# Letting three kinds of small products in a mixing phase wait for company on TensorE

## The chip, the cores and the metric

The kernel runs on one core of one Trainium2 chip, in one launch. The metric is device time in microseconds (us), as the median of several executions. The engines are named as in the profile: PE is TensorE, DVE is VectorE, ACT is ScalarE, POOL is GpSimd, SP is SyncE, which issues most DMAs. PEld is the load of a matrix product's stationary operand, which runs beside PE.

## The reference

Two layers of a diffusion backbone over 256 context and 512 latent tokens (768 columns together), with a model width of 1024, in float32. Each layer has a mixing sub-layer and a squared-ReLU MLP. Cut to what matters:

```
h = modulate(rmsnorm(x))
conv, q, k, v, rw, gate = split(h @ w_in)          # 7552 output channels
y_att  = differential attention(q, k, v)           # 4 heads
y_conv = silu(layernorm(depthwise_conv31(glu(conv))))
y_rw   = rwkv7(rw)                                 # 8 heads of 64, two directions
m = g1*(y_conv@p_conv) + g2*(y_att@p_att) + g3*(y_rw@p_rwkv);  x += gl1 * (m @ w_out)
x += gl2 * (square(relu(modulate(rmsnorm(x)) @ mlp_w1)) @ mlp_w2)
```

The RWKV-7 branch is a recurrence over tokens with a 64x64 state for each head and direction:

```
sa = s @ (-kk_t);  s = s * w_t + sa (kk_t * a_t)^T + v_t k_t^T;  y_t = s @ r_t
```

Its per-token decay w and rate a come from two low-rank products (64 rows in, 128 channels out).

## The kernel before, in words

**Wide products.** Every dense matrix is cut into units of 128 output channels. A float32 product is made of three products of rounded parts (weights `wh`, `wl`; activations `hh`, `hl`), all 128x128 stationary with 512 columns (latent) or 256 columns (context), into tiles called `mmps`. ACT makes `wh` from the loaded `wr`, DVE makes `wl`. Where this text counts wide products, one of 256 columns counts half.

**The recurrence, in chunks of 64 tokens.** For each of four head pairs and two halves of the tokens, `half_prep` makes decays and rates from the low-rank products (tiles `lps` and `aps`, two products each, of 64 rows). `half_t` makes the products that are masked into triangles (`tps`, three groups of eight per half, 64 rows). `inverse` takes the triangles through DRAM and inverts 16x16 blocks on DVE; `half_solve` joins the blocks to inverses of 64x64 (`wps`, `jps`, products of 32x32). `half_tok` transposes operands (`trps`, `vps`) and makes the value products (`tvps`, three groups of eight per half, 64x64). `chain_piece` then walks the chunks in order: `ca`, `cb` and `psy` are its small products (128x64 and 64x64), and each step waits for ACT and DVE between its products. All of these stand in PE's one queue, between wide products.

**What sets the order.** The program is written out engine by engine by a planner at build time. Each piece of work is a Python generator that yields the time at which its next instruction could start, its engine, and sometimes a lock on PSUM slots (`"bb"` wants both) and a time bonus. `weave` asks all open generators, takes the one with the earliest possible start, and adds the instruction's estimated cost to that engine's clock (`spend`). Ties go to the generator named first in an order string; in a mixing phase the wide products (`G`) stand behind the chain, preparation and token work. So a group of small products that was ready went in at the next boundary between two wide products.

**Stages of a layer.** The mixing phase (`phase_a`) runs until chain, inverse, preparation and token work have ended; wide products of the input projection fill PE meanwhile. Then attention (`attend`) follows: scores `sps`, softmax on DVE and ACT, transposes `atps`, values `mmps<-aat`, a norm over `ash`/`asl`, the result split in `yah`/`yal`. What is left of the input projection (the gates last) fills PE there. In layer 0 the convolution's 124 taps (`cacc`, on DVE) run in and behind attention, in layer 1 in the mixing phase. Then come the merges (`ya`, `y`, `yc` times the p matrices), `w_out` and the MLP. In layer 0 much of the gates is left for the time behind attention; in layer 1 the last of the input projection ends with attention.

Of the kernel before, what the change touches and what calls it, by code (L numbers as in the profile page):

```python
# [19 lines left out]
P = 128  # L20
# [31 lines left out]
SPARE = 1.5  # L52
EPS = 0.02
STICK = 0.2
BLK = 1040
CTX = (0, NCTX)
LAT = (NCTX, NLAT)
# [63 lines left out]
class Trunk:  # L121
# [105 lines left out]
    def product(self, out, lhsT, rhs, at=None, beside=0, **kw):  # L227
        self.nc.tensor.matmul(out, lhsT, rhs, **kw)  # L228
        m, n = lhsT.free_size(), rhs.free_size()
        c = n if rhs.dtype == F32R else 4 * n * max(m, 32) / P  # L230
        cost = (max(0.027, c / 2400) + 0.003) if not beside else 0.004
        if rhs.dtype != F32R:
            cost = max(cost, 0.1 if m == P else 0.0) + (0.012 if 32 < n <= P else 0.04 if n > P else 0.0)
        if self.short and m == P:
            cost += 0.06
        self.short = cost < 0.1
        return self.spend("PE", cost, at)

    def turn(self, out, src):
        self.nc.tensor.transpose(out, src, self.ident)  # L240
        return self.spend("PE", 0.119)

    def load(self, out, in_, q=None, rate=360e3):
# [39 lines left out]
    def weave(self, order, streams, until=None):  # L283

        todo = self.todo
        todo += [[g, 0.0, "PE", None, None, 0.0, k] for k, g in streams.items()]
        todo.sort(key=lambda s: order.find(s[6]) % 99)  # L290
        while todo and not (until and until()):
            best, at = None, 0.0
            for s in todo:
                held, names = self.held(s[4])
                if held is None or s[3] and not s[3]():
                    continue
                t = max(s[1], self.clock[s[2]] + s[5], held) - s[5]
                if best is None or t < at - EPS:
                    best, at, got, since = s, t, names, held
            assert best, "no stream can go on"  # L300
            self.t0 = max(best[1], since)
            self.now = max(self.now, at)
            self.got = got[0] if got else None
            for k in got:
                self.locks[k] = None
            try:
                y = next(best[0])
            except StopIteration:
                todo.remove(best)
                continue  # L310
            best[1:6] = y + (None, None, 0.0)[len(y) - 2:]
# [100 lines left out]
    def start(self):  # L412
        self.queues, self.closing, self.n_queued = [], False, 0
        self.plan, self.after, self.after_over, self.n_after = [], deque(), False, 0
        self.n_load = self.n_conv = self.n_used = 0
        self.banks = dict(lat=deque([0.0, 0.0]), ctx=deque([0.0]))
        self.ring = dict(lat=deque([self.mm, self.mm]), ctx=deque([self.mm]))
        self.gone = dict(lat=deque(), ctx=deque())
        self.raws, self.parts = deque([self.wp] * WR), deque([self.wp] * WC)
        self.locks, self.t0, self.now, self.todo, self.short = {}, 0.0, 0.0, [], False  # L420
        self.shared, self.shared_t = 0, 0.0

    def enqueue(self, i, q):
# [550 lines left out]
    def half_prep(self, l, p, hh):  # L974
# [8 lines left out]
        t3 = max(pp["kk_t"], pp["r_t"], pp["lw_t"], self.ready["lw"], self.ready["la"])  # L983
        late = bk[:, 1].rearrange("p c x t -> p (c x t)")
        low = []
        for i, (name, src) in enumerate((("e1", self.lw), ("a", self.la))):
            yield t3, "PE", None, "bb"
            pss = self.both_slots("lps" if i == 0 else "aps")
            for d in range(2):
                rows = slice(64 * d, 64 * d + 64)  # L990
                e = self.product(pss[d][:, 0:N], pp["lora_w"][rows, i, :], src[rows, u0:u0 + N], beside=d, start=True, stop=True)
            for d in range(2):
                yield e, "ACT"
                x = late[:, N * i:N * i + N] if d else pr.tile([P, N], F32, tag=name, name=name)
                o = 8 * i + 4 * d + p
                t = S.activation(out=x, in_=pss[d][:, 0:N], func=AF.Tanh, scale=0.5, bias=self.wa0[:, o:o + 1])
                self.free(f"b{d}", t)
                low.append((x, t))
        for d in range(2):
# [48 lines left out]
            t3 = V.tensor_tensor(out=bet, in0=q64(a), in1=q64(e3), op=ALU.mult)  # L1048
# [3 lines left out]
            for tok, n, more in add:  # L1052
# [7 lines left out]
                if more:  # L1060
                    t = V.tensor_tensor(out=dst, in0=dst, in1=src, op=ALU.add)
                else:
                    t = S.activation(out=dst, in_=src, func=AF.Copy)
# [3 lines left out]
    def half_t(self, n, pp, hh, prep, c0):  # L1067
        pr, V = self.pr, self.V
        ar, bk, pc, ready = prep
        ta = pr.tile([P, 6, 2, 2, 64], F32, tag="ta", name="ta", bufs=2)  # L1070
        trs = []

        def masked(b, ps, pi, h, e, tr):

            yield e, "DVE"
            t = V.tensor_tensor(out=ta[:, 2 * pi:2 * pi + 2, h, :, :], in0=ps[:, :, :, 0:64],
                                in1=self.mask[:, 0:1, :].unsqueeze(1).to_broadcast([P, 2, 2, 64]), op=ALU.mult)
            if tr is not None:
                yield e, "DVE"
                t = V.tensor_tensor(out=tr[:, :, :, h, :].rearrange("p c g t -> p (c g) t"),  # L1080
                                    in0=ps.rearrange("p c g t -> p (c g) t")[:, :, 64:128],
                                    in1=self.mask[:, 1, :].unsqueeze(1).to_broadcast([P, 4, 64]), op=ALU.mult)
            self.free(b, t)
            return t

        for pi in range(3):
            need_y = 128 * (3 * hh + pi) >= c0
            nx = 2 if need_y else 1
            tr = pr.tile([P, 2, 2, 2, 64], F32, tag="tr", name="tr", bufs=6 if c0 == 0 else 4) if need_y else None
            trs.append(tr)  # L1090
            yield ready, "PE", None, "bb"
            pss = [x.rearrange("p (c g t) -> p c g t", c=2, g=2) for x in self.both_slots("tps")]
            for cc in range(2):
                c = 2 * pi + cc
                for d in range(2):
                    g = 1 - (cc ^ d)
                    for h in range(2):
                        hs = slice(64 * h, 64 * h + 64)
                        e = self.product(pss[h][:, cc, g, 0:64 * nx], bk[hs, d, c].rearrange("p x t -> p (x t)"),
                                         ar[hs, d, c, 0:nx].rearrange("p x t -> p (x t)"), beside=h, start=True, stop=True)  # L1100
            for h in range(2):
                t = yield from masked(f"b{h}", pss[h], pi, h, e, tr)
        sc, sc2 = self.blk_in[self.blk % 2], self.blk_out[self.blk % 2]
        self.blk += 1

        def blocks(x):
            return x.rearrange("(p x) -> p x", x=BLK)[:, 0:1024].rearrange("p (i w) -> p i w", w=64)[:, :, 0:16]

        def rows(x, g):
            return x[g * 48 * BLK:(g + 1) * 48 * BLK].rearrange("(n y) -> n y", y=4 * BLK)[:, 0:4096].rearrange(  # L1110
                "n (s t) -> s n t", t=64)

        yield t, "SP"
        for g in range(2):
            td = self.load(rows(sc, g), ta[64 * g:64 * g + 64, :, :, g, :].rearrange("p c h t -> p (c h) t"), rate=180e3)
        for d in range(2):
            for x in range(2):
                tb = self.G.tensor_tensor(out=bk[:, d, :, x, :], in0=bk[:, d, :, x, :],
                                          in1=pc[:, d, :].unsqueeze(2).to_broadcast([P, 6, 64]), op=ALU.mult)
        j = pr.tile([P, 6, 2, 64], F32, tag="j", name="j", bufs=2)  # L1120
        st = dict(hh=hh, ta=ta, bk=bk, ar=ar, pc=pc, trs=trs, toks=[], tok_t=[], gvs=[], tvs=[], j=j, pp=pp, bk_t=tb, ta_t=t)
        self.inverses.append((st, td, lambda x=sc: blocks(x), lambda x=sc2: blocks(x), lambda g, x=sc2: rows(x, g)))
        return st
# [28 lines left out]
    def half_tok(self, st, pi):  # L1152
# [9 lines left out]
        t = S.activation(out=tok.rearrange("p d c t -> p (d c t)"), in_=ps, func=AF.Copy)  # L1162
# [12 lines left out]
        t = S.activation(out=gv[64:128, 1:3, :], in_=pv[64:128], func=AF.Copy)  # L1175
        st["gvs"].append(gv)
        self.free(b, t)
        yield t, "PE", None, "bb"
        pss = [self.rwe.tile([P, 512], F32, tag=f"b{g}", name="tvps", bufs=1) for g in range(2)]
        for cc in range(2):  # L1180
            for h in range(2):
# [9 lines left out]
        for g in range(2):  # L1191
            gr = slice(64 * g, 64 * g + 64)
            t = S.activation(out=tv[gr].rearrange("p c t -> p (c t)"), in_=pss[g][gr, 0:256], func=AF.Copy)
# [1050 lines left out]
```

## Time and profile before

| | |
|---|---|
| median of 3 runs | 2925.59 us (2921.22 to 2925.92) |
| the profiled execution's own time | 2913.63 us |
| its span, first to last instruction | 2911.8 us |
| PE busy | 2768.5 us, 95% of the span |
| DVE busy | 1961.5 us, 67% |
| ACT busy | 1299.9 us, 45% |
| mean granted TensorE clock | 0.986 |

The profiled execution took 12 us less than the median of the timed runs, so differences are worked out against 2913.63 us and then carried over to the median. A busy share is that of the whole span; the stages have different limits. PE's busy time counts a product from its start to the end of its pipeline, so what a product costs is read from the distance between the starts of two neighbours.

### The profile page before, as it was taken

What the parts mean: (1) busy time and instruction counts of PE and PEld (TensorE: products, weight loads), DVE (VectorE), ACT (ScalarE), POOL (GpSimd) and SP (SyncE); (2) the same over time, 40 slices, a digit from 0 to 9 for tenths busy, and PEclk for the clock granted to TensorE, in tenths of its full rate; (3) what the DMA queues carried; (4) which work ended last, traced back from release to release, by engine and by line L of the source; (5) the groups of instructions that cost most, each with busy time, mean ns of one, the idle gap of its engine ahead of it and who ended that gap; (6) DMA issues with size and microseconds to landing.
All of it is one profiled execution on the core that took longest, in us unless ns stands there. A gap on an engine that the chain in (4) does not pass through costs nothing.

```text
span 2911.8 us, 56372 instructions
## 1 busy us (share of the span) xinstructions
PE 2768.5 (95%) x22423; PEld 2229.7 (77%) x22423; DVE 1961.5 (67%) x4311; ACT 1299.9 (45%) x2522; POOL 104.9 (4%) x181
## 2 busy tenths in 40 slices
PE   8999999999999999999999999999999888899998
PEld 6777777777788887888888777777777656788887
DVE  6778787489995548764333569889985667644445
ACT  4556655455544224231313356556554653433333
POOL 0000000011000000000000000000000100000000
PEclk9999999999999999999999999999999999999999
DMA  5232223354237633553112223223245535322223
GB/s 210 65 77 70 74 79 90 115 151 127 72 124 271 242 119 120 183 186 101 63 62 69 96 70 86 66 83 83 73 120 155 146 119 160 130 97 96 95 95 104
DMA packets 247751, 330.96 MB, mean 114 GB/s; under 512 B 118256, under 2 KB 124032, under 8 KB 247360
## 3 DMA queue, kind: packets, MB, share of 16 engines
q1 hardware_dynamic: 242160, 311.63, 33.6%
q0 software_dynamic: 3712, 14.17, 2.0%
q8 instruction: 176, 2.88, 0.4%
q10 hardware_dynamic: 1616, 1.56, 0.2%
q14 instruction: 87, 0.71, 0.1%
HBM read 266.32 MB, written 47.60 MB: 108 GB/s over the span
## 4 chain that ended last, share of the span: by engine, by line
PE 73%; DVE 14%; ACT 4%; DMA 3%; issue 2%; SPq 0%; DVEq 0%; POOL 0%; ACTq 0%; POOLq 0%
PE mmps L228 60%; PE ca L228 3%; DVE cacc L92 2%; DVE wl L92 2%; DVE ast L92 2%; PE tps L228 1%; ACT wh L92 1%; PE psy L228 1%; PE jps L228 1%; PE wps L228 1%; PE tvps L228 1%; DVE ap L92 1%; DVE x L92 1%; PE atps L240 1%; PE sps L228 1%
## 5 line engine op out<-in xcount | busy, mean ns | idle before, releaser
L228 PE MATMUL mmps<-hh,wh 128*128 128x512 f32 (+1 forms) x2344 | 850.0, 363 | 22.1 <-DVE k L92 5.7
L228 PE MATMUL mmps<-hh,wl 128*128 128x512 f32 (+1 forms) x2344 | 843.3, 360 | 6.0 <-DVE wl L92 5.9
L228 PE MATMUL mmps<-hl,wh 128*128 128x512 f32 (+1 forms) x2344 | 843.6, 360 | 4.3 <-DVE hl L92 4.1
L92 DVE TENSOR_TENSOR wl<-wr,wh 128x512 fp32r<-128x512 f32 x596 | 412.2, 692 | 473.9 <-ACT wh L92 460.1
L92 ACT ACTIVATE wh<-wr 128x512 fp32r<-128x512 f32 x596 | 375.2, 630 | 707.6 <-PE mmps L228 656.9
L228 PEld LDWEIGHTS mmps<-hh,wh 128*128 128x128 f32 x2344 | 446.9, 191 | 93.4 <-issue 18.1
L228 PEld LDWEIGHTS mmps<-hh,wl 128*128 128x128 f32 x2344 | 446.1, 190 | 77.1 <-DVE wl L92 12.8
L228 PEld LDWEIGHTS mmps<-hl,wh 128*128 128x128 f32 x2344 | 447.3, 191 | 67.5 <-DVE hl L92 7.4
L228 PE MATMUL mmps<-ffl,wh 128*128 128x512 f32 (+1 forms) x792 | 279.3, 353 | 0.0
L228 PE MATMUL mmps<-ffh,wh 128*128 128x512 f32 (+1 forms) x792 | 278.1, 351 | 0.0
L228 PE MATMUL mmps<-ffh,wl 128*128 128x512 f32 (+1 forms) x792 | 277.1, 350 | 0.0
L92 DVE SCALAR_TENSOR_TENSOR cacc<-upad,dww,cacc 128x783 f32<-128x783 f32 (+1 forms) x240 | 215.1, 896 | 4.3
L228 PEld LDWEIGHTS mmps<-ffh,wh 128*128 128x128 f32 x792 | 149.1, 188 | 22.7
L228 PEld LDWEIGHTS mmps<-ffh,wl 128*128 128x128 f32 x792 | 148.9, 188 | 21.5
L228 PEld LDWEIGHTS mmps<-ffl,wh 128*128 128x128 f32 x792 | 149.4, 189 | 20.8
L92 DVE SCALAR_TENSOR_TENSOR x<-mmps,mod,x 128x512 f32<-128x512 f32 (+1 forms) x126 | 80.1, 636 | 46.2 <-PE mmps L228 44.8
L92 POOL TENSOR_TENSOR bk<-bk,pc 128x384 f32<-128x384 f32 x64 | 57.4, 927 | 1200.0 <-PE tps L228 1138.5
L92 DVE SCALAR_TENSOR_TENSOR sq<-mmps,rl 128x512 f32<-128x512 f32 x96 | 56.9, 596 | 40.0 <-ACT rl L92 39.9
L92 ACT ACTIVATE stage<-mmps 128x512 f32<-128x512 f32 (+1 forms) x116 | 59.1, 510 | 51.7 <-PE mmps L228 48.7
L92 ACT ACT_TABLE_LOAD x62 | 79.5, 1283 | 4.2 <-PE mmps L228 2.1
L92 ACT ACTIVATE rl<-mmps 128x512 f32<-128x512 f32 x96 | 49.3, 514 | 67.9 <-PE mmps L228 67.9
L92 DVE TENSOR_REDUCE ast<-sps 128x1 f32<-128x768 f32 (+1 forms) x80 | 67.5, 844 | 17.3 <-PE sps L228 17.3
(317 smaller groups left out, 4377.1 us busy)
## 6 DMA issues: line engine op xcount, KB each, us to landing
wr<-in_w_dram SPq DMA_DIRECT2D x268, 256.0 KB, 2.5
wr<-in_win_dram SPq DMA_DIRECT2D x236, 256.0 KB, 2.7
modw<-in_modw_dram SPq DMA_DIRECT2D x80, 512.0 KB, 4.6
wr<-in_pw_dram SPq DMA_DIRECT2D x48, 256.0 KB, 2.9
wr<-in_wo_dram SPq DMA_DIRECT2D x44, 256.0 KB, 2.6
g<-stage SPq DMA_DIRECT2D x24, 384.0 KB, 3.2
gate<-g SPq DMA_DIRECT2D x24, 384.0 KB, 3.8
scb<-in_modw_dram SPq DMA_DIRECT2D x16, 512.0 KB, 6.5
```

The lines of the kernel that those rows point to most:

```text
L92: f(**kw)
L228: self.nc.tensor.matmul(out, lhsT, rhs, **kw)
L240: self.nc.tensor.transpose(out, src, self.ident)
```

## The change

A new constant `DEFER = 1.5` (us). The three places that ask for both PSUM slots for low-rank (`lps`, `aps`), masked (`tps`) and value (`tvps`) products now yield `-DEFER` as their bonus. For a negative bonus `weave` takes the possible start as the ready time if PE's last planned product was a small one (`self.tiled`: fewer than 128 rows or columns of the stationary operand), and as the ready time plus 1.5 us otherwise. A wide product or a transpose clears `self.tiled`. A group that is late for any other reason by 1.5 us goes in as before. No instruction is added or removed by the diff itself; the planner writes another order.

```diff
+DEFER = 1.5
...
         self.short = cost < 0.1
+        self.tiled = m < P or lhsT.shape[0] < P
         return self.spend("PE", cost, at)
...
         self.nc.tensor.transpose(out, src, self.ident)
+        self.tiled = False
...
-                t = max(s[1], self.clock[s[2]] + s[5], held) - s[5]
+                if s[5] < 0:
+                    t = max(s[1] - (0.0 if self.tiled else s[5]), self.clock[s[2]], held)
+                else:
+                    t = max(s[1], self.clock[s[2]] + s[5], held) - s[5]
...
-            yield t3, "PE", None, "bb"
+            yield t3, "PE", None, "bb", -DEFER
...
-            yield ready, "PE", None, "bb"
+            yield ready, "PE", None, "bb", -DEFER
...
-        yield t, "PE", None, "bb"
+        yield t, "PE", None, "bb", -DEFER
```

**Place 1: PE, mixing phase of layer 0, the low-rank products of the fifth half (third head pair).** Before:

```order
L228 MATMUL tvps<-gv,ta 64x64 x8
L228 MATMUL mmps<-hh_177,wl 128x512
L228 MATMUL mmps<-hh_179,wh 128x512
L228 MATMUL mmps<-hl_180,wh 128x512
L228 MATMUL mmps<-hh_179,wl 128x512
L228 MATMUL lps<-lw,loraw 128x384 x2
L228 MATMUL mmps<-hh_181,wh 128x512
L228 MATMUL mmps<-hl_182,wh 128x512
```

With the change:

```order
L229 MATMUL mmps<-hh_177,wl 128x512
L229 MATMUL ca<-x_702,ar 64x128 x2
L229 MATMUL psy<-tr,gv 64x64
L229 MATMUL psy<-ar,x_701 64x64
...
L229 MATMUL lps<-lw,loraw 128x384 x2
L229 MATMUL ca<-rhs,j 64x64
L229 MATMUL cb<-rhs,j 64x64
...
L229 MATMUL mmps<-hh_179,wh 128x512
```

The low-rank pair stood alone between wide products and now stands inside a step of the chain.

**Place 2: PE, the end of attention in layer 1.** `aat` is the last value product, `ash`/`asl` the sum for the last head's norm, `yah` the first merge product. Before:

```order
L228 MATMUL mmps<-aat,avt 128x512 x6
L228 MATMUL mmps<-hl_17324,wh 128x512
L228 MATMUL mmps<-hh_17323,wl 128x512
L228 MATMUL mmps<-hh_17325,wh 128x512
L228 MATMUL mmps<-hl_17326,wh 128x512
L228 MATMUL mmps<-hh_17325,wl 128x512
L228 MATMUL mmps<-ash,onesr 128x512
L228 MATMUL mmps<-asl,onesr 128x512
L228 MATMUL mmps<-yah_25362,wh 128x512
```

With the change:

```order
L229 MATMUL mmps<-hh_17317,wh 128x512
L229 MATMUL mmps<-hl_17318,wh 128x512
L229 MATMUL mmps<-ash,onesr 128x512
L229 MATMUL mmps<-asl,onesr 128x512
L229 MATMUL mmps<-hh_17317,wl 128x512
L229 MATMUL mmps<-hh_17319,wh 128x512
...
L229 MATMUL mmps<-hl_17326,wh 128x512
L229 MATMUL mmps<-hh_17325,wl 128x512
L229 MATMUL mmps<-yah_25321,wh 128x512
```

Between the last value product and `ash` there were 5 wide products and are 16; between `asl` and the first merge product there were none and are 13. The 24 more are one unit of the gates that was planned ahead of attention before.

**Place 3: ACT, layer 0, between the last chunk of the chain and the first scores.** `stage` empties a wide product's PSUM bank, `ysq<-sums` is a logarithm, and the table loads switch between it and the other functions. Before:

```order
L92 ACT_TABLE_LOAD
L92 ACTIVATE stage<-mmps 128x512
L92 ACT_TABLE_LOAD
L92 ACTIVATE ysq<-sums,eps 128x256
L92 ACT_TABLE_LOAD
L92 ACTIVATE stage<-mmps 128x256
L92 ACTIVATE ysq<-ysq 128x768
L92 ACTIVATE wh<-wr 128x512
```

With the change:

```order
L93 ACTIVATE stage<-mmps 128x512
L93 ACT_TABLE_LOAD
L93 ACTIVATE ysq<-sums,eps 128x512
L93 ACTIVATE aqh<-aqk 128x768
L93 ACTIVATE sumh<-ysq 128x256
L93 ACT_TABLE_LOAD
L93 ACTIVATE stage<-mmps 128x256
L93 ACTIVATE wh<-wr 128x512
L93 ACT_TABLE_LOAD
L93 ACTIVATE ysq<-sums,eps 128x256
L93 ACTIVATE wh<-wr 128x512
```

The two `stage` copies now stand one table load earlier each, and two weight copies `wh` stand ahead of the last loads.

## Rows read from the trace of the kernel before

**Rows 1.** Windows by stage: us, PE, PEld, DVE, ACT, POOL busy, PEclk, DMA, GB/s.

```profile
85.00:560.00 475.00, 460.46 (x6322) 361.94 (x6321) 351.26 (x1040) 264.41 (x587) 30.11 (x48) 1.00 0.29 78
560.00:851.00 291.00, 269.87 (x1451) 217.85 (x1450) 257.30 (x432) 161.08 (x310) 18.91 (x36) 0.98 0.36 114
851.00:1084.00 233.00, 228.61 (x1699) 193.95 (x1699) 135.62 (x214) 77.88 (x126) 0.00 (x0) 1.00 0.63 219
1708.00:2213.00 505.00, 488.49 (x6065) 365.61 (x6065) 436.80 (x1162) 273.42 (x591) 33.27 (x48) 1.00 0.30 84
2213.00:2395.00 182.00, 157.72 (x682) 114.09 (x679) 115.34 (x211) 107.40 (x196) 18.55 (x36) 0.96 0.50 148
```

**Rows 2.** Timeline of PE in layer 0's mixing phase: start, us, what, idle.

```profile
295.69 0.39 PE L228 MATMUL mmps<-hl,wh 128*128 128x512 f32 x1
295.92 0.40 PE L228 MATMUL mmps<-hh,wl 128*128 128x512 f32 x1
296.24 0.92 PE L228 MATMUL lps<-lw,loraw 64*128 64x384 f32 x4
297.09 0.50 PE L228 MATMUL mmps<-hh,wh 128*128 128x512 f32 x1
297.43 0.40 PE L228 MATMUL mmps<-hl,wh 128*128 128x512 f32 x1
```

**Rows 3.** Timeline of PE, chain steps followed by a wide and by a masked group.

```profile
205.20 0.22 PE L228 MATMUL cb<-rhs,j 64*64 64x64 f32 x1
205.35 0.38 PE L228 MATMUL mmps<-hh,wh 128*128 128x256 f32 x1
...
209.41 0.22 PE L228 MATMUL cb<-rhs,j 64*64 64x64 f32 x1
209.46 0.22 PE L228 MATMUL ca<-rhs,j 64*64 64x64 f32 x1
209.47 0.22 PE L228 MATMUL cb<-rhs,j 64*64 64x64 f32 x1
209.62 1.16 PE L228 MATMUL tps<-ar,bk 64*128 64x128 f32 x16
```

**Rows 4.** Timeline of PE at the end of attention in layer 1.

```profile
2385.91 0.80 PE L228 MATMUL mmps<-hl,wh 128*128 128x512 f32 x1
...
2388.84 0.50 PE L228 MATMUL mmps<-ash,onesr 128*128 128x512 f32 x1 [1.20 <-ACT ash L92]
2389.56 0.50 PE L228 MATMUL mmps<-asl,onesr 128*128 128x512 f32 x1 [0.22 <-DVE asl L92]
...
2391.76 0.40 PE L228 MATMUL mmps<-yah,wl 128*128 128x512 f32 x1
2394.74 0.51 PE L228 MATMUL mmps<-yah,wh 128*128 128x512 f32 x1 [2.59 <-ACT yah L92]
```

**Rows 5.** Timeline of PE ahead of attention in layer 0.

```profile
576.33 0.38 PE L228 MATMUL mmps<-hh,wh 128*128 128x256 f32 x1 [2.99 <-ACT stage L92]
...
581.18 0.79 PE L228 MATMUL mmps<-hh,wl 128*128 128x512 f32 x1 [2.25 <-DVE wl L92]
```

**Rows 6.** Timeline of ACT at the same place.

```profile
572.82 1.28 ACT L92 ACT_TABLE_LOAD   x1
...
574.60 1.28 ACT L92 ACT_TABLE_LOAD   x1
```

**Rows 7.** Window behind those waits, columns as in the first group.

```profile
577.60:584.40 6.80, 4.55 (x15) 3.18 (x14) 5.83 (x9) 1.85 (x3) 2.05 (x4) 0.52 0.80 254
```

**Rows 8.** Groups by line, whole span: count, busy us, mean ns, idle before.

```profile
L228 PE MATMUL jps<-j,jt 32*32 32x32 f32 x2304 | 36.3, 193 | 6.3 <-issue 3.6 <-DVE jt L92 2.3 <-ACT jt L92 0.2
L228 PE MATMUL wps<-jt,ta 32*32 32x32 f32 x2304 | 32.2, 193 | 6.9 <-DVE jt L92 6.0 <-DVE jp L92 0.4 <-DVE tr L92 0.3
L92 DVE TENSOR_TENSOR wl<-wr,wh 128x512 fp32r<-128x512 f32 x596 | 412.2, 692 | 473.9 <-ACT wh L92 460.1
L92 DVE SCALAR_TENSOR_TENSOR cacc<-upad,dww,cacc 128x783 f32<-128x783 f32 (+1 forms) x240 | 215.1, 896 | 4.3
```

More of the change, by code (lines that the diff above doesn't have):

```diff
@@ L419, in start @@
         self.raws, self.parts = deque([self.wp] * WR), deque([self.wp] * WC)
-        self.locks, self.t0, self.now, self.todo, self.short = {}, 0.0, 0.0, [], False
+        self.locks, self.t0, self.now, self.todo, self.short, self.tiled = {}, 0.0, 0.0, [], False, False
         self.shared, self.shared_t = 0, 0.0
```

## The prediction

> **What bounds the kernel now.** I read the windows by stage first [rows 1]. In both mixing phases (85 to 560 us and 1708 to 2213 us) PE is busy for 460.5 of 475 us and 488.5 of 505 us, so only 14.5 and 16.5 us are idle; behind attention in layer 0 (851 to 1084 us) 4.4 us are. The two attention stages are looser: 21.1 us idle in layer 0 (560 to 851 us, with DVE busy for 257.3 of 291 us beside it) and 24.3 us in layer 1 (2213 to 2395 us). Where PE is full, two things count: time that it loses between products while busy, and idle time that is merely moved. The timeline of PE shows the first. Wide products of 512 columns follow each other at 0.23 us (295.69 to 295.92), but the last one ahead of a lone low-rank group takes 0.32 us to the group's start, and the first one behind it takes 0.34 us to its successor [rows 2]. Chain products on 64x64 start 0.01 and 0.05 us apart (209.41, 209.46, 209.47), but 0.15 us pass from the last of them to the next wide product (205.20 to 205.35) [rows 3]. So a lone visit to small products costs PE about 0.09 + 0.11 + 0.11 = 0.31 us beyond its work.
>
> **What the change moves.** Every engine keeps its work, apart from two more table loads on ACT and a few copies that change between ACT and DVE; ACT is not full in any stage [rows 1]. What differs is the order. I counted four things over PE's whole order, before and with the change. (a) Unbroken runs of small products fall from 395 to 380. Of the 128 deferred groups, those with no other small kind beside them make 71 runs before and 63 with the change, so most still wait out their 1.5 us in vain. (b) Passages from one small shape straight to another rise from 107 to 118. (c) Wide products planned up to the chain's last product fall from 1150 to 1118 in layer 0 and by 24 in layer 1, because a mask group inside a step of the chain fills a gap that wide products filled, and no longer delays a step that is ready. (d) In layer 0, 86 wide products stood between the chain's end and the first scores and 110 do now; 648.5 stood within attention and 579 do now; the rest goes behind it. Layer 1's attention is the same row for row up to its end (place 2).
>
> **Term 1, the joins: -3.4 us.** 15 fewer visits at 0.31 us are 4.7 us. 11 more passages between small shapes give back 0.11 to 0.12 us each, 1.3 us: from a 64x64 product to a mask product 0.15 us pass (209.47 to 209.62), as many as to a wide one [rows 3].
>
> The Trainium skill, TensorEngine Tiling (Array Packing), section Tiling Modes, states that a change of tiling mode, not just of tile, drains TensorE. By that rule a mask or low-rank group, whose mode is none of the chain's, saves little by standing beside the chain; the trace agrees, with the same 0.15 us [rows 3]. Without the rule this term would be -4.7 us.
>
> **Term 2, the end of attention in layer 1: -4.0 us.** PE waits 1.20 us for `ash`, 0.22 us for `asl` and 2.59 us for the last head's `yah`, with nothing left to fill [rows 4]. The 24 products that no longer stand ahead of attention stand there now: 24 x 0.23 = 5.5 us of work. The 16 ahead of `ash` end at about 2385.9 + 0.6 + 15 x 0.23 = 2390.0, some 1.2 us after `ash` is ready, and the 13 behind `asl` with the nine merge products that stood there already (the last of them at 2391.76) make 22 x 0.23 = 5.1 us, which is the 5.2 us from 2389.56 to 2394.74. So 5.5 us leave the mixing phase and some 1.3 us come back at the end. The three waits add up to 4.0 us, the most that this term can give; the least is nothing, if the last head's chain on ACT and DVE gets later by as much as it is covered.
>
> **Term 3, ahead of attention in layer 0: -5.0 us.** Two waits of 2.99 and 2.25 us lie there [rows 5]. The first is for a PSUM bank that the `stage` copies empty, which stood behind table loads of 1.28 us each [rows 6]. The second is for a `wl` on DVE that stood behind a product with `ysq`, which ACT had made late. In the new order each `stage` copy is one table load earlier (place 3), and both `wl` stand ahead of that DVE product. Behind the waits the granted clock is 0.52 [rows 7], so most of 6.8 us were at the lower of the two levels, 1.2 GHz. The 4.6 us that PE was busy in there would have cost up to 2.3 us less at 2.4 GHz. The most is thus 5.2 + 2.3 = 7.5 us, the least nothing, if the waits form again at other table loads. The stretch itself is set by loads and rotations of q and k, so 24 more wide products at 0.23 us, 5.5 us, must find room there; I take 5.0.
>
> **Term 4, attention in layer 0: +2.6 us.** 69.5 fewer wide products are 16.0 us less for PE there, and they come back behind attention, where PE is full. The stage shrinks by as much only if DVE lets it. Up to the 45th of the 48 score tiles' rows of maxima, 71 taps stood in DVE's order and 62 do now, and there are about four `wl` fewer (one for each 18 wide products): 9 x 0.896 + 4 x 0.692 = 10.8 us [rows 8]. The other 5.2 us may show as idle time; I take half of it, with 0 and 16.0 as ends.
>
> **Not costed.** Idle time within the mixing phases (31 us together) is taken as unchanged: the order puts 39 and 31 fewer wide products between the same steps, but deferred groups have taken their places. The deferral itself costs nothing where PE has wide products, and it always has in these stages: what is queued behind a late mask group is its masks on DVE, the trip through DRAM and the solve; the first solve of layer 0 stands 17 wide products later (3.9 us), the eighth 28 earlier.
>
> **Sum.** -3.4 - 4.0 - 5.0 + 2.6 = -9.8 us. From 2913.6 us the profiled execution would go to 2903.8 us. The median stands 12.0 us above it, so 2915.8 us, 0.33% less.
>
> **Rivals.** A measurement of this kernel can tell about 0.2% (5.9 us) from no change, that is below 2919.7 or above 2931.4 us.
>
> *Only the joins count.* The waits of terms 2 and 3 dissolve in the order, but on the chip the new order meets other late copies and loads of the same size. For it: every wait behind a table load is one that the plan did not foresee. Against it: 24 spare products at the end of layer 1 are a fact of the order. Time: 2925.6 - 3.4 = 2922.2 us, the same. Chance 0.20.
>
> *Attention in layer 0 keeps its length.* DVE is busy for 88% of that stage [rows 1]; if its softmax sets the pace, the 16.0 us taken from PE turn to idle time and come back in full behind it. Then +16.0 replaces +2.6: 2929.2 us, the same. Against it are the taps that leave. Chance 0.10.
>
> *The solves wait: slower.* A mask group that waits 1.5 us makes everything up to the solve later. PE waited 6.9 and 6.3 us at `wps` and `jps`, mostly for DVE's `jt` [rows 8], so this path has no slack in some of the 16 halves. The order puts fewer wide products between the last mask group and the solve in eight of them. If these eight lose 2 us each, 16 us come on top: 2931.8 us. It decides from there: the idle time at `wps` and `jps` must rise from 13.2 to about 29 us. Against it: the other eight got more room, and the chain ends earlier in the order. Chance 0.12.
>
> **How the numbers follow.** My forecast, some 10 us less, gets 0.58. Its own range is 2910 us (term 3 in full, term 4 at nothing: -14.9) to 2919. The range for 8 in 10 goes down to 2906, since the clock can also gain at waits that I have not counted, and up to 2929, so that the first two rivals are in. Faster 0.60 (the forecast and a lucky part of the rivals), same 0.28, slower 0.12.
>
> **What would show it.** Term 1: chain and mask groups side by side in PE's timeline, 0.15 us between shapes. Term 2: no wait above 1 us between the last `aat` and the first merge products, and first scores of layer 1 some 7 us earlier against layer 1's own start. Term 3: the two waits ahead of the first scores and the low clock behind them gone. Term 4: idle time of PE between first score and last transpose of layer 0 within 3 us of before. I am wrong if the idle time of the mixing phases moves by more than 5 us either way, above all at `wps` and `jps`, or if new low-clock stretches stand where none were.

## The result: 2939.5 us, slower by 0.55%

The kernel with the change takes 2939.52 us (median of 6 runs, 2928.20 to 2941.32), the kernel before 2921.47 us (6 runs, 2918.04 to 2925.92). The ratio is 1.0055, 95% interval 1.0037 to 1.0073: slower by more than the 0.2% that can be told, where 0.33% less was forecast. The forecast had started from a median of three runs, 2925.59 us; the six runs put it 4 us lower. The profiled execution took 2941.32 us (span 2939.2 us) at a mean granted clock of 0.976, for 0.986 before.

The windows by stage of the changed kernel, in the order of [rows 1] (layer 0: mixing, up to the last `ash`, behind it; layer 1: mixing, up to the last head's `yah`). Columns: window, length, busy us of PE, PEld, DVE, ACT, POOL (x instructions), PEclk, DMA share, GB/s.

```profile
88.70:555.70 467.00, 451.81 (x6259) 355.04 (x6257) 350.75 (x1038) 264.44 (x587) 29.28 (x48) 1.00 0.28 74
555.70:842.90 287.20, 262.68 (x1404) 210.73 (x1404) 237.87 (x411) 158.47 (x305) 18.58 (x36) 0.98 0.38 117
842.90:1094.90 252.00, 245.40 (x1794) 208.70 (x1794) 155.75 (x236) 81.53 (x134) 0.00 (x0) 1.00 0.60 208
1720.80:2232.60 511.80, 494.76 (x6020) 368.86 (x6019) 431.32 (x1156) 269.88 (x587) 30.77 (x48) 0.96 0.29 80
2232.60:2417.20 184.60, 163.18 (x713) 118.79 (x708) 116.17 (x212) 108.88 (x199) 18.78 (x36) 0.95 0.50 144
```

Layer 0's mixing phase is 8 us shorter, its attention only 4 us, and the stretch behind it 19 us longer. Layer 1's mixing phase should have lost some 8.5 us (31 wide products at 0.23 us and its share of the joins) and is 7 us longer, with the granted clock at 0.96 of full speed where it was at 1.00. There are two losses, then, one in each layer.

**The clock in layer 1.** PE's timeline at the solve of the fifth half (start, us, engine and line, operation, tiles, shape; in brackets the idle time before it and what ended it):

```profile
2029.40 0.39 PE L229 MATMUL mmps<-hh,wh 128*128 128x512 f32 x1
2029.63 0.40 PE L229 MATMUL mmps<-hl,wh 128*128 128x512 f32 x1
2029.87 0.39 PE L229 MATMUL mmps<-hh,wl 128*128 128x512 f32 x1
2030.90 0.36 PE L229 MATMUL sums<-sumh,bonesr 128*128 128x256 f32 x1 [0.64 <-DVE tr L93]
2031.09 0.28 PE L229 MATMUL sums<-suml,bonesr 128*128 128x256 f32 x1
2032.42 0.24 PE L229 MATMUL wps<-jt,ta 32*32 32x32 f32 x2 [1.05 <-DVE ksq L93]
2032.85 1.49 PE L229 MATMUL wps<-jt,ta 32*32 32x32 f32 x94 [0.18 <-DVE tr L93]
2034.83 2.20 PE L229 MATMUL jps<-j,jt 32*32 32x32 f32 x96 [0.49 <-ACT jt L93]
2038.80 0.79 PE L229 MATMUL mmps<-hh,wh 128*128 128x512 f32 x1 [1.78 <-ACT upad L93]
...
2039.82 0.63 PE L229 MATMUL mmps<-hh,wl 128*128 128x512 f32 x1
2040.25 0.63 PE L229 MATMUL mmps<-hh,wh 128*128 128x512 f32 x1
```

From 2029.87 to 2038.80 us PE starts no 128x512 product: two short sums, the 32x32 products of the solve, and five waits. Behind that wide products start 0.43 us apart (2039.82 to 2040.25), before it 0.23 us. The windows around the place give the clock:

```profile
2022.50:2032.50 10.00, 7.33 (x43) 5.11 (x41) 9.35 (x18) 2.95 (x5) 4.02 (x6) 1.00 0.44 120
2032.50:2053.00 20.50, 17.98 (x326) 11.86 (x327) 12.03 (x28) 9.14 (x17) 0.00 (x0) 0.51 0.25 58
2053.00:2063.00 10.00, 10.00 (x95) 7.17 (x95) 8.96 (x34) 6.84 (x17) 0.00 (x0) 0.99 0.19 68
```

For 20.5 us PE ran at 0.51, the lower of its two levels, 1.2 GHz; by an estimate, half of the 18.0 us that PE was busy in there, 9.0 us, is what the lower level cost. Two more such stretches, of 10.2 us each, begin at 1967.6 and 2206.6 us, both at a solve. In all, PE was low for 41.0 us of this phase, before for 3.4 us. ACT's timeline shows part of why the solve stood open for so long:

```profile
2030.71 1.28 ACT L93 ACT_TABLE_LOAD   x1
...
2034.30 0.99 ACT L93 ACTIVATE jt<-wps 32x384 f32<-32x384 f32 x2 [1.05 <-PE wps L229]
2035.30 1.28 ACT L93 ACT_TABLE_LOAD   x1
...
2038.15 0.60 ACT L93 ACTIVATE upad<-mmps 128x512 f32<-128x512 f32 x1
```

Two table loads fall within it, and the `upad` copy that frees a bank for the next wide product stands behind the second. In the order of before, the same solve has wide products ahead of `wps`, between `wps` and `jps`, and behind:

```profile
2012.33 0.39 PE L228 MATMUL mmps<-hh,wh 128*128 128x512 f32 x1
2012.65 1.02 PE L228 MATMUL wps<-jt,ta 32*32 32x32 f32 x96
2013.60 0.50 PE L228 MATMUL mmps<-hl,wh 128*128 128x512 f32 x1
...
2015.66 1.32 PE L228 MATMUL jps<-j,jt 32*32 32x32 f32 x96
2016.92 0.39 PE L228 MATMUL mmps<-hh,wh 128*128 128x256 f32 x1
```

There the longest time without a start of a wide product, in the whole mixing phase, is 4.1 us; here it is 8.9 us. Ahead of the other two falls the starts of wide products are at most 2.7 us apart, so what brings those is open.

**The solves themselves** hardly wait longer: 15.7 us of idle time in all, 13.2 before [rows 8].

```profile
L229 PE MATMUL jps<-j,jt 32*32 32x32 f32 x2304 | 39.0, 198 | 9.0 <-issue 4.8 <-DVE jt L93 2.3 <-ACT jt L93 1.2
L229 PE MATMUL wps<-jt,ta 32*32 32x32 f32 x2304 | 34.0, 196 | 6.7 <-DVE jt L93 3.9 <-DVE tr L93 1.1 <-DVE ksq L93 1.1
```

**The end of attention in layer 1** [rows 4]. PE's, SP's and ACT's timelines:

```profile
2410.87 0.40 PE L229 MATMUL mmps<-ash,onesr 128*128 128x512 f32 x1
...
2417.23 0.49 PE L229 MATMUL mmps<-yah,wh 128*128 128x512 f32 x1 [0.65 <-ACT yah L93]
2418.04 0.50 PE L229 MATMUL mmps<-yal,wh 128*128 128x512 f32 x1 [0.32 <-DVE yal L93]
...
2425.86 0.50 PE L229 MATMUL mmps<-yah,wh 128*128 128x512 f32 x1 [1.49 <-ACT wh L93]
2427.71 0.50 PE L229 MATMUL mmps<-yah,wl 128*128 128x512 f32 x1 [1.11 <-DVE wl L93]
```

```profile
2416.16 0.33 SPq L248 DMA_DIRECT2D g<-stage  x1
...
2418.85 1.37 SPq L248 DMA_DIRECT2D yrf<-yr  x3
```

```profile
2423.27 0.63 ACT L93 ACTIVATE yh<-yrf 128x512 fp32r<-128x512 f32 x1 [4.06 <-DMA yrf<-yr]
...
2425.20 0.61 ACT L93 ACTIVATE wh<-wr 128x512 fp32r<-128x512 f32 x1
```

The forecast waits are filled: 4.0 us are 1.0 us. But the unit that fills them is stored last (2416.16), the load of `yrf` follows it on SP's queue, ACT stands 4.06 us at `yh`, and the `wh` behind it lets PE wait for 1.49 and 1.11 us instead. Before, that load was issued 3.1 us ahead of the first `yah` product (2394.74); now it is issued 1.6 us behind it:

```profile
2391.61 1.37 SPq L245 DMA_DIRECT2D yrf<-yr  x3
```

**Ahead of attention in layer 0** [rows 5], the longest waits left are these, and the granted clock stays full:

```profile
581.78 0.50 PE L229 MATMUL mmps<-hh,wh 128*128 128x512 f32 x1 [0.49 <-ACT wh L93]
...
590.28 0.38 PE L229 MATMUL sps<-akl,aqh 128*128 128x256 f32 x1 [0.75 <-DMA akl<-akl]
```

### The profile page after: what moved, and what is told of

The parts are those of the page before. It is cut to its first block, busy times and chain, and to the rows that moved or that the text cites. A ratio compares the mean times of both kernels' runs of the same rounds, so it can differ in the third digit from the quotient of the medians.

```text
span 2939.2 us, 56353 instructions
## 1 busy us (share of the span) xinstructions
PE 2790.7 (95%) x22423; PEld 2246.6 (76%) x22423; DVE 1959.6 (67%) x4310; ACT 1298.7 (44%) x2525; POOL 101.5 (3%) x181
```

## The experiments

The theory at first: layer 1 loses by the clock next to its solves (A1), layer 0 by wide products that left attention and came back behind it (A2). The rivals: the deferral's own waits, or a clock that falls by chance. In the expected texts, theory A is A1, and from E6 on A1 and A2 together; B and C are what each text says.

Ratios are against the kernel before, run on the same chip. "Clock" is the mean granted clock over the timed runs of that version, with the difference from those of before beside it. The last column needs a word. Runs of one and the same kernel differ by up to 20 us (before: 2915 to 2935 us), and those with a lower mean clock are longer. A straight line through all 221 timed runs, with a level for each version, one for the kernel before on each chip, and one common slope, gives 19.7 us for each 0.01 of clock, with a scatter of 2.5 us. The column is the level against before's: an estimate of what is left when the clock is taken out.

| | median us (runs) | ratio, 95% interval | clock | left, us |
|---|---|---|---|---|
| E1 layer 0 alone | 2932.64 (12) | 1.0036 [1.0023, 1.0048] | 0.9812 (-0.0023) | +5.0 |
| E2 layer 1 alone | 2932.06 (12) | 1.0028 [1.0015, 1.0041] | 0.9783 (-0.0052) | -2.0 |
| E3 idle products, three halves | 2937.90 (6) | 1.0055 [1.0038, 1.0072] | 0.9803 (-0.0032) | +9.2 |
| E4 the change again | 2939.07 (6) | 1.0057 [1.0038, 1.0076] | 0.9780 (-0.0055) | +5.8 |
| E5 idle products, one half | 2938.07 (10) | 1.0038 [1.0023, 1.0054] | 0.9799 (-0.0029) | +6.7 |
| E6 value products alone | 2929.62 (12) | 1.0012 [0.9998, 1.0027] | 0.9799 (-0.0029) | -2.0 |
| E7 0.5 us | 2938.73 (7) | 1.0037 [1.0023, 1.0050] | 0.9800 (-0.0028) | +7.2 |
| E8 6 us | 2989.98 (5) | 1.0206 [1.0188, 1.0223] | 0.9692 (-0.0136) | +35.5 |
| E9 layer 0 alone, 1.2 us | 2926.62 (12) | 1.0006 [0.9994, 1.0018] | 0.9822 (-0.0004) | +1.2 |
| E10 1.2 us | 2940.08 (6) | 1.0049 [1.0034, 1.0064] | 0.9788 (-0.0038) | +6.1 |
| E11 without mask products | 2939.36 (6) | 1.0051 [1.0037, 1.0065] | 0.9782 (-0.0044) | +5.2 |
| E12 without value products | 2950.82 (6) | 1.0095 [1.0077, 1.0112] | 0.9760 (-0.0066) | +12.8 |
| E13 order of before, idle products | 2922.48 (12) | 1.0001 [0.9990, 1.0012] | 0.9831 (+0.0005) | +1.9 |
| E14 E2 with idle products | 2929.00 (11) | 1.0023 [1.0014, 1.0031] | 0.9805 (-0.0021) | +2.3 |
| E15 E2 again | 2931.19 (6) | 1.0030 [1.0018, 1.0041] | 0.9780 (-0.0046) | -0.6 |

**E1 and E2, one layer at a time.** At the three places:

```diff
-            yield t3, "PE", None, "bb", -DEFER
+            yield t3, "PE", None, "bb", -DEFER * (self.l == 0)
```

and `(self.l == 1)` for E2.

> The deferral acts in layer 0 alone; layer 1 keeps the order of before, row for row. Theory A (the loss is TensorE's clock, which falls in layer 1's mixing phase where the new order puts waits and small products together): some 3 to 9 us slower than before, all of it ahead of 1095 us, and layer 1's mixing phase is back at 504 us with under 10 us at the lower clock. Rival B (the loss is that attention in layer 0 keeps its length while its wide products come back behind it): 10 to 18 us slower, the whole loss. Rival C (the deferral costs wherever it acts): about half of the loss, 9 us.

> The deferral acts in layer 1 alone; layer 0 keeps the order of before, row for row. Theory A: 10 to 17 us slower, with 30 to 45 us at the lower clock in layer 1's mixing phase (41 us in the changed kernel's profile, 3.4 us before) and that phase at 508 to 515 us instead of 504. Rival B: no slower than before, even some 6 us faster by the waits filled at the end of layer 1's attention. Rival C: about 9 us slower.

The two losses (0.36% and 0.28%) together are about the change's (0.55% and 0.57%), and by the last column they differ in kind: on balance layer 1's is all clock, layer 0's about half. With E1 layer 1's mixing phase takes 503.3 us with no low clock, with E2 506.4 us with 27.3 us of it. By the times alone rival C, some 9 us for each layer, came nearest (9.9 and 9.3 us between the medians), and theory A's 3 to 9 and 10 to 17 us were both just missed. Against C as waits speaks that idle time in the mixing phases hardly moved (table below), and in layer 0 E9.

**E3 to E5, idle products at the solves.** To the change, ahead of each `wps` and `jps` block of three halves in layer 1 (E3: the fourth, fifth and eighth), or of those of the first of two levels of one half (E5: the fifth, shown above); their results are written over. E5's edit (E13 and E14 have the same; the expected text of E13 calls that level the last):

```diff
+    def fill(self, st, ps, lvl):
+        if self.l == 1 and st["n_half"] == 4 and lvl == 32:
+            for k in range(4):
+                self.nc.tensor.matmul(ps[:, 0:384], self.ones_r, self.h[k][0][:, NCTX:NCTX + 384], start=True, stop=True)
...
+            self.fill(st, pss[-1], lvl)
```

> The changed kernel, with four idle products of 384 columns (0.16 us each) put ahead of each wps and jps block of three halves of layer 1, those next to which the clock fell at 1967.6, 2032.5 and 2206.6 us. They are written over, so the result stands; they are 48 products, 7.9 us of work, part of it inside waits. Theory A: the clock stays up in layer 1's mixing phase, up to 19 us come back there against 2 to 6 us of added work, so 8 to 15 us faster than the changed kernel. Rival (the clock falls whatever fills the waits, or the falls cost little): 3 to 8 us slower than the changed kernel.

> The changed kernel once more, for a second profile and a time on the same chip as the three others. Theory A: 0.4 to 0.7% slower than before, and again 25 us or more at the lower clock in layer 1's mixing phase. If the falls of the clock were chance of one execution, that phase has under 15 us of it here, and the time is as slow all the same.

> The changed kernel with idle products (written over, so the result stands) ahead of the first wps and jps block of one half alone, the fifth of layer 1, where PE had waits of 1.05 and 0.49 us and the clock then stayed low for 17 to 20 us: 8 products, 1.3 us of work, most of it inside those waits. Theory A (falls of the clock next to the solves are what layer 1 loses): the fall at 2032 us is gone or under 7 us long, the mixing phase of layer 1 is 3 to 8 us shorter than in the changed kernel (510 to 512 us), and the time lies between it and before. Rival (the falls just move to the next solve): that phase is within 2 us of the changed kernel's.

Low clock in layer 1's mixing phase: 34.1 us with E4, 10.2 with E3, 13.7 with E5; the phase takes 510.2, 505.7 and 502.5 us. At the fifth half's solve the low clock lasts 17.1 us with E4 (20.5 us in the profile above), and 3.4 us with E3 and E5; at the fourth half's, 6.8 us with E4, none with E3, which has idle products there, and 10.2 us with E5, which has none. E3 has 6.8 us at the first half's solve, where E4 and E5 have none. So idle products made falls shorter where they were put, and did not always end them. In the whole time E3 missed A1's 8 to 15 us: it is 1.2 us faster than E4; by the table the clock gave 4.5 us, and its many products took 3.4 us of them back. E5 and E4 ran on different chips, and their intervals overlap. This called for E13 to E15.

**E6 to E8, another choice or size of the deferral.** E6 leaves the bonus at the `tvps` place alone; E7 and E8 set

```diff
-DEFER = 1.5
+DEFER = 0.5
```

and `6.0`.

> Only the value products (tvps) may wait. By my count of PE's order the joins are those of the changed kernel (380 runs of small products, 118 passages between shapes: -3.4 us), the wide products in the two mixing phases 1007 and 1133 (955 and 1102 with the whole change, 994 and 1133 before), and those in layer 0's attention 617.5 (579 and 648.5). Theory A (a loss by clock and by attention in layer 0, not by the joins): 0 to 6 us slower than before, with under 20 us at the lower clock in layer 1's mixing phase. Theory C (each deferred group costs time by being late): a third of the loss, 5 to 6 us.

> DEFER is 0.5 us instead of 1.5. Fewer runs of small products are left than with 1.5 (369 against 380, and 395 before; 126 passages between shapes), so the joins are worth 5.9 us; the fill in layer 0's attention is as in the changed kernel (579). Theory A: attention in layer 0 keeps its length again (255 to 259 us), so layer 0 loses 5 to 9 us; layer 1 depends on where its clock falls. Theory C: a third of the loss, 6 us. If joins were what counts, it would be faster than before by 3 us or more.

> DEFER is 6 us. 354 runs of small products are left and 143 passages between shapes, so the joins are worth 8.6 us, but each group that finds no company is 6 us late: 1150 and 1250 wide products stand in the mixing phases (994 and 1133 before), which must be longer by some 25 to 30 us each, and attention has that much less to fill it. Theory A: what PE loses is its idle time and its clock; attention in both layers shows 5 us or more of new idle time each, and the kernel is 10 us or more slower than before. If joins were what counts: 5 us or more faster.

E6 makes the same joins by the count, and its -2.0 us without the clock is near the -3.4 us that they should give; the clock took 0.0029. E7 has only 3.4 us of low clock in layer 1's mixing phase and still loses 0.37%, where C had a third of the loss: 715 wide products (value and norm products counted in) stand between first `sps` and last `ash` in layer 0 with it, as with the change (778 before), and the stretch behind takes 253.3 us. It also has 52 wide products fewer in layer 1's attention and 51 more in the mixing phase ahead, which takes 515.3 us. So the clock isn't the whole loss. E8 joins most of all and is worst: layer 0's mixing phase holds 1150 wide products for 994 and takes 515.3 us, its attention keeps 261.4 us. A chain that ends late carries wide products into the mixing phase, and they are missing where waits could use them.

**E9 to E12, other orders with attention in layer 0 as full as before.** E9 is E1 with `DEFER = 1.2`, E10 the change with 1.2; E11 takes the bonus from `tps`, E12 from `tvps`:

```diff
-            yield ready, "PE", None, "bb", -DEFER
+            yield ready, "PE", None, "bb"
```

> The bonus stands in layer 0 alone, with 1.2 us in place of 1.5 us. Its order in layer 0's mixing phase is close to that of the version with 1.5 us in layer 0 alone (971.5 wide products for 955, 166 runs of small products for 165), but 648.5 wide products stand within layer 0's attention as before the change, for 579. Theory A (layer 0 lost time because wide products that left attention came back behind it in full): 7 us less than that version's 1.0036, a ratio of 1.0000 to 1.0018, and layer 0 between the last ash and the first rps at 234 us, not 253, with attention at 260 us. Theory B (layer 0 lost it by the deferral itself, by clock and by later solves): the ratio stays at 1.003 to 1.004.

> The change with DEFER = 1.2 in both layers: 372 runs of small products and 127 passages between small shapes (a saving of 4.8 us by the prediction's price of the joins), 648.5 wide products in layer 0's attention, 65 more wide products in layer 1's mixing phase than before and as many fewer in its attention. Theory A: nothing of layer 0's loss, and layer 1 as its clock falls: 1.000 to 1.003. Theory B: 1.004 and more. If the mean granted clock of the timed runs stays at 0.983, as before, the time falls by the joins, 0.998.

> Low-rank and value products are deferred by 1.5 us, mask products not: 375 runs and 122 passages (-4.5 us by the joins), 648.5 wide products in layer 0's attention as before. Theory A: the layer-0 loss is gone, so that only clock falls stand against the joins: 0.999 to 1.002. Theory B (any deferral clusters small products next to the solves and the clock falls there): 1.003 to 1.005, with a mean granted clock of the timed runs of 0.978.

> Low-rank and mask products are deferred by 1.5 us, value products not: 378 runs and 122 passages (-3.5 us by the joins), 648.5 wide products in layer 0's attention. Theory A: 0.999 to 1.002. Theory B: 1.003 to 1.005. Of the versions with and without mask products, the one with a lower mean granted clock of its timed runs holds the groups that bring the falls.

E9 came out as A2 said: 1.0006 for E1's 1.0036. The windows of the two, attention and the stretch behind it, E1 first:

```profile
593.70:851.90 258.20, 233.75 (x1233) 186.39 (x1232) 220.85 (x383) 139.82 (x277) 13.91 (x27) 0.97 0.34 100
851.90:1104.60 252.70, 247.75 (x1794) 210.90 (x1794) 155.60 (x236) 81.56 (x134) 0.00 (x0) 0.99 0.62 207
```

```profile
595.00:860.20 265.20, 245.97 (x1319) 198.89 (x1319) 240.83 (x402) 143.32 (x283) 14.23 (x27) 0.97 0.34 102
860.20:1096.60 236.40, 230.87 (x1700) 195.32 (x1699) 136.20 (x214) 78.31 (x127) 0.00 (x0) 0.99 0.64 216
```

63 wide products more cost attention 7.0 us, and 71 fewer save 16.3 us behind it. E10 and E11 missed theory A's ratios and came out at theory B's (1.0049 and 1.0051), but not where E11's text has the clock fall, next to the solves: their low clock is 6.8 and 13.7 us in layer 1's mixing phase, and 44.4 and 41.0 us in its attention (10.2 us before). What I had counted but not priced: 72 and 76 wide products left layer 1's attention, most of them for the mixing phase, which takes 516.2 and 525.2 us, and attention got no shorter. E10's window of it:

```profile
2259.20:2414.30 155.10, 123.84 (x482) 84.91 (x480) 95.51 (x179) 83.84 (x159) 14.15 (x27) 0.86 0.41 114
```

31.3 us without PE, at 0.86 of the clock: the loss of layer 0, once more, in the other layer. E12, far above both of its ranges, is E8's case on a smaller scale (1083 wide products in layer 0's mixing phase, 506.9 us, 21.2 us idle for 14.5). Its clock is the lowest of the three, but as its order differs everywhere, that doesn't place the falls in the mask products.

**E13 to E15, the idle products again, with a control.** E15 is E2; E14 adds E5's edit to it; E13 puts E5's edit into the order of before (`-DEFER * 0`).

> The order of before, with 4 idle products of 384 columns ahead of each of the two block solves of the last level (wps, jps) of the fifth half of layer 1: 8 more products, at 0.16 us each 1.3 us of work. A control: by the theory that layer 1 loses time at low clock next to these solves only in the order of the change, the mean granted clock of the timed runs stays within 0.0005 of before's and the ratio is 1.0000 to 1.0008. If idle products raise the clock in any order, the clock rises here too and the ratio falls under 1.

> The change in layer 1 alone, with the same 8 idle products. If a good part of layer 1's loss is low clock next to these two solves: the mean granted clock of the timed runs rises by 0.002 to 0.003 against the version without them on the same chip, and the ratio falls by 0.001 to 0.0015 (4 to 6 us at 20 us for each 0.01 of clock, less 1.3 us of work). If the low clock only moves to other places or is spread: clock and ratio stay, the ratio rises by 0.0005.

> The change in layer 1 alone, again, for the comparison on the same chip: 1.0015 to 1.0041, a mean granted clock of the timed runs of about 0.978, and low clock next to the solves of layer 1 in the profile.

PE's timeline at the place, E15 and then E14:

```profile
2028.94 0.24 PE L229 MATMUL wps<-jt,ta 32*32 32x32 f32 x2 [1.05 <-DVE ksq L93]
2029.37 1.08 PE L229 MATMUL wps<-jt,ta 32*32 32x32 f32 x94 [0.18 <-DVE tr L93]
...
2032.07 1.48 PE L229 MATMUL jps<-j,jt 32*32 32x32 f32 x90 [0.34 <-DVE jt L93]
2034.94 0.80 PE L229 MATMUL mmps<-hh,wh 128*128 128x512 f32 x1 [1.40 <-ACT upad L93]
```

```profile
2030.44 0.86 PE L1207 MATMUL wps<-hh,onesr 128*128 128x384 f32 x4
2031.65 0.24 PE L229 MATMUL wps<-jt,ta 32*32 32x32 f32 x2 [0.35 <-DVE ksq L93]
2032.08 1.08 PE L229 MATMUL wps<-jt,ta 32*32 32x32 f32 x94 [0.18 <-DVE tr L93]
2034.78 0.97 PE L1207 MATMUL jps<-hh,onesr 128*128 128x384 f32 x4 [1.62 <-DVE jt L93]
```

The windows of 20 us from the solve on, E15 and then E14:

```profile
2028.90:2048.90 20.00, 17.26 (x357) 12.20 (x357) 15.71 (x43) 11.71 (x23) 0.00 (x0) 0.83 0.32 79
```

```profile
2031.60:2051.60 20.00, 16.81 (x375) 12.01 (x375) 16.82 (x45) 12.65 (x24) 0.00 (x0) 1.00 0.31 80
```

The fall is gone, with the waits still there (1.62 us for `jt`; from the one ahead of `sums` to the next wide product the waits add up to 4.2 us, in E15 to 4.4). Over the timed runs the clock rose by 0.0025, as expected; the control, in the order of before, moved by 0.0005. The time fell by 2.2 us, less than the expected 4 to 6 and within the two intervals: 4.9 us from the clock by the slope, 2.9 us given back (1.3 us of it the products' own work). So for this place A1 is shown for the clock, and for the time only by the slope: it carries about half of layer 1's loss of clock (0.0046 to 0.0052).

That the order brings this fall, and not chance, shows over the profiles. In the four with the change's order of layer 1 and no idle products (the change, E2, E4, E15) the clock falls here each time, for 6.8 to 20.5 us, behind 8.6 to 8.9 us without a start of a wide product; in the four with the order of before (before, E1, E9, E13) it never does. At the fourth half's solve it is the same four against none. The fall at the eighth half's stands in two of the four (the change, E4) and not in the two others, so there chance has a part. And the phase is as long as its low clock says: 511.8, 510.2, 506.4 and 503.2 us with 41.0, 34.1, 27.3 and 20.5 us of it (the change, E4, E2, E15), 501.4 us with 10.2 us (E14). Whether missing wide products or the waits between the small ones let the clock fall was not tested apart: the idle products also cut the wait for `ksq` from 1.05 to 0.35 us. No version here is faster than the kernel before.

## Why the prediction was wrong, step by step

The stretches between marks in PE's timeline, as means over profiles with the same order of the layer: in layer 0 before, E2, E13, E14 and E15 against the change, E1, E3, E4 and E5; in layer 1 before, E1, E9 and E13 against the change, E2, E4 and E15.

| stretch, us | order of before | of the change | difference |
|---|---|---|---|
| layer 0: first `lps` to last `psy` | 475.7 | 468.6 | -7.1 |
| to the first `sps` | 31.7 | 33.2 | +1.5 |
| to the last `ash` | 260.5 | 257.0 | -3.5 |
| to the first `rps` behind it | 236.3 | 252.7 | +16.4 |
| layer 1: first `lps` to last `psy` | 504.1 | 507.9 | +3.8 |
| to the first `sps` | 29.0 | 28.8 | -0.2 |
| to the last `ash` | 147.0 | 150.6 | +3.6 |
| to the first `ych` product | 62.6 | 65.5 | +2.9 |

The eight differences add up to +17.4 us.

**Term 1, the joins: the sign fits, the size isn't shown.** E6, with the same count of joins, left -2.0 us without the clock, E2 -2.0 and E15 -0.6 us for the 1.4 us of layer 1 (6 visits fewer, 4 passages more). The estimate is uncertain by a us or more and holds what else those orders changed, so it says no more than the sign.

**Term 2, the end of layer 1's attention: failed at "1.3 us come back at the end".** The waits were filled, but from first `sps` to `ych` the stretch is 6.5 us longer for 5.5 us more work: all of it came back. PE's idle time in it fell by 0.8 us, not by 4.0: the filling unit made a store and loads late that ACT and then PE wait for, and the wait for `ych` behind it stayed (9.83 us before, 9.81 after). Some 2.2 us of the 6.5 are the clock (half of PE's busy time at the lower level rose from 5.8 to 8.0 us).

**Term 3, ahead of layer 0's attention: right.** 24 more wide products, 5.5 us, lengthen the stretch by 1.5 us: 4.0 us gained, 5.0 forecast.

**Term 4, attention in layer 0: the step "the stage shrinks by as much only if DVE lets it" failed.** DVE's work between first `sps` and last `ash` fell by 19.5 us (240.7 to 221.2), more than the 10.8 us I had, and the stage shrank by 3.5 us, not 13.4. So DVE's sum of work didn't set the pace. In the means, PE lost 63 wide products there, 14.5 us; 7.6 us of that came as idle time (16.4 to 24.0 us, where the text wanted it within 3), and some 2.6 us as lower clock (low for 7.5 and 15.7 us). PE's longest waits are now 5.2 us for `ash` and 2.9 us for the load of `akl`; which link of scores, softmax and values decides isn't settled. The 16.4 us behind, for 71 wide products more, came as forecast. The term is +12.9, not +2.6: the second rival, with 0.10, nearly to its size.

**"Not costed: idle time within the mixing phases" is where the largest loss lay.** The idle time did stay (before and after: 14.5 and 15.2 us in layer 0, 16.5 and 17.0 us in layer 1), as the step said; it failed in taking nothing else there to move. What moved was the speed of busy time. I costed low clock only where a wait would go (term 3), and never where an order takes wide products from between small ones. Layer 1's mixing phase lost 14.2 us by it, for 0.9 us (half the busy time at the lower level, means as in the table). Without these 13.3 us the phase would be 9.5 us shorter, near the 8.5 us that 31 fewer wide products and 1.4 us of joins make. In layer 0 the same phase lost 2.0 us by the clock and 1.2 us by idle time, so that it gained 7.1 us for the 11 us of its 39 wide products and its joins. The text named low clock as what would make it wrong, but gave it no case. Its sign of first scores some 7 us earlier in layer 1 came out at 3.6 us later.

**The third rival** named the place, the solves, but not the mechanism: their idle time went to 15.7 us and not to 29.

Summed, -9.8 us, 10.3 us more for term 4, 5.2 us for term 2 (6.5 us came back, not 1.3) and 13.3 us for layer 1's clock make +19; the two medians differ by 16 to 18 us.

## What to carry to other kernels

Where a planner fills the waits of one stage with work of another, moving that work is not free in either direction: taken out of a stage that hardly gets shorter by it, it comes back in full elsewhere (here 63 wide products less shortened attention by 3.5 us, and 71 more behind it cost 16.4 us). Joining small products saves tenths of a microsecond each (0.31 us by the prediction), and one fall of the clock cost more than ten times that (an estimated 9.0 us at the solve above); so look at where wide products stay between the small ones, and at the mean granted clock of several runs, and not at PE's idle time alone.

## What was not expected of the hardware

The granted clock falls where no wait is long: ahead of the fall at 2032.5 us PE had done two short sums and begun the 32x32 products, with waits of 0.64 and 1.05 us. With eight products of 384 columns without any use, 1.3 us of work, it stayed at 2.4 GHz there in E14; in E5, and in E3 with more of them, it was low for 3.4 us, against 6.8 to 20.5 us without. The Trainium skill, TensorE: Matmul & The Clock Gate, section "A second HAM failure mode: psum-queue depth-cycling", tells of a kernel in which short idle times between groups of products make the clock go back and forth; the trace agrees in part: the idle times around the fall are short, 0.18 to 1.78 us, but E14 has waits of 0.18 to 1.62 us at the same place and no fall.

The clock also differs between executions of the same rows: ahead of the first `lps` PE was at 1.2 GHz for 10.2 us in one execution of before, and for 23.9 us in E13's, whose rows up to there are the same. A mean granted clock lower by 0.01 goes with about 20 us in this kernel, so one profile's clock isn't enough to compare two versions.
